# One accumulator instead of two for the routed experts: two scatter-adds in a row per expert tile

## The chip, the core and the metric

The kernel runs on one core of one Trainium2 chip. The core has a matmul engine (TensorE, PE in the rows, with its weight loads as PEld), a vector engine (VectorE, DVE), an activation engine (ScalarE, ACT), GpSimd (POOL) and SyncE (SP), which here only issues transfers. Sixteen DMA engines move data between the chip's memory (DRAM) and the on-chip memory (SBUF). Each engine runs its own instructions in order, and waits for others by semaphores. The metric is the device time of one execution in microseconds (us); less is better.

## The reference, cut to what matters

A backbone of two layers over 256 context and 256 latent tokens, D = 1024. Each layer has a token mixer and then a channel mixer: a shared expert for every token and 64 routed experts, of which each token goes to 8. Layer 0 routes all 512 tokens, layer 1 only the 256 latent ones, so 4096 and 2048 pairs of a token and an expert.

```python
TOP_K = 8; N_EXPERTS = 64; EXPERT_HIDDEN = 256

def swiglu(x, wg, wu, wd):
    return (jax.nn.silu(x @ wg) * (x @ wu)) @ wd
...
    # for every block of up to MOE_BLOCK rows of one expert e
    def block_ffn(args):
        tok, wt, e = args
        return swiglu(h_pad[tok], w_gate[e], w_up[e], w_down[e]) * wt[:, None]
    yb = lax.map(block_ffn, (...))
    return jax.ops.segment_sum(yb.reshape(n_rows, d), row_tok, num_segments=t + 1)[:t]
...
    routed = routed_experts(h, eidx, wts.astype(h.dtype), w_exp_gate, w_exp_up, w_exp_down)
    return routed + swiglu(h, w_sh_gate, w_sh_up, w_sh_down)
...
    h_lat = layer_norm(DN_ALPHA * h_lat + g2 * y_lat, ln2_g[l], ln2_b[l])
```

## The kernel before

Everything is float32. Outside of the routed experts a scheduler places the instructions of each engine; `experts` is written under a manual schedule, so its order is the order of the code.

**Routing** (`route`, L1240 on). The rows of an expert are cut into units of 64 rows, and two units make a tile of 128 rows. The first unit lies in partitions 0 to 63 (lane 0), the second in 64 to 127 (lane 1). A unit has as many rows with a token as its expert has left, up to 64; the others are empty. Tables give for each row of each tile the token to gather (`t_gather`) and the row of the accumulator to add to (`t_scatter`). The two units of a tile can hold the same token, for two experts. So the accumulator `acc` in DRAM has two halves of n + 64 rows, one for each lane. Row 0 to n - 1 of the first half are written by the shared expert (L980); the rest is filled with zeros from `zt` by transfers on ACT's queue (L1262). Empty rows add to spare rows, so that all 128 indices of a scatter are different and all are moved.

**The expert loop** (`experts`). For tile t, `body(t)` emits: transposes of the hidden values of tile t - 1 (`h_t`, L1586), gate and up products of tile t (L1577), the copies of the next weights out of a ring of four slots (`copies_gu` L1546, `copies_dn` L1552, on VectorE), the activation (L1581), transposes of the next tile's rows (`x_t`, L1568), the gather of tile t + 3 on GpSimd (L1526), and `down(t - 1)`: the down products (L1594), two ScalarE copies into `y` scaled by the routing weight (L1596), and a scatter-add of `y` into `acc` on GpSimd (L1597). There are two `y` buffers, used in turn, so `y` of tile t can be written once the scatter of tile t - 2 has landed. SyncE loads the next expert (three loads of 1 MB, L1227) when a slot is free, and signals landed loads (L1239).

All indirect transfers are GpSimd's, on queue q0; expert weights are on q1. A scatter-add reads its destination, so each waits until the scatter ahead of it has landed.

**The combine** (`combine`, L1643 on). For each 128 tokens SyncE loads both halves of `acc` (L1673), GpSimd adds them (L1675), VectorE multiplies and adds the residual (L1676, L1678), and a layer norm follows. In layer 0 the next mixer waits for it; in layer 1 it is the end of the program.

Of the kernel before, what the change touches and what calls it, by code (L numbers as in the profile page):

```python
# [60 lines left out]
def shape_consts():  # L61
# [6 lines left out]
    cols = [p]  # L68
    for n in (T, NLAT):
        pm, ln = p % UNIT, p // UNIT  # L70
        cols += [1 + n + pm, ln * (n + UNIT) + n + pm]
# [29 lines left out]
class Build:  # L101
# [37 lines left out]
    def rstd(self, pool, var, n, scale=1.0):  # L139
        """(scale * var + eps) ** -0.5 for [P, n]"""  # L140
        nc = self.nc
        ve = pool.tile([P, n], F32, name="rs_ve", bufs=4)
        nc.vector.tensor_scalar(ve, var, scale, LN_EPS, op0=ALU.mult, op1=ALU.add)  # L143
        r = pool.tile([P, n], F32, name="rs_r", bufs=6)
        nc.gpsimd.tensor_tensor(r, ve, self.eps[:, 1:2].to_broadcast([P, n]), op=ALU.pow)  # L145
        return r

    def ln_stats(self, pool, x, width):
        """rstd and -mean*rstd of x [P, width]"""
# [17 lines left out]
    def ln_sums(self, pool, x, sm, junk=None):  # L167
        """minus mean and rstd of x [P, D] from its sums"""
# [14 lines left out]
    def ln_two(self, pool, x, sm, g, b, out, total=None):  # L183
        """(x - mean) * rstd * g + b over [P, D], its sums to total"""
# [6 lines left out]
    def mod_prepare(self):  # L191
        """silu(c) of both streams, transposed: csT [P, KC, 32], column 0 context, 1 latent"""
# [20 lines left out]
    def mod_steps(self, l, i, rp, pool, bank):  # L213
        """columns 2048 i .. of silu(c) w_mod + b_mod; round 0 stays on chip transposed, the others go to DRAM"""
# [3 lines left out]
        for hf in range(2):  # L218
            # 256 columns to 32 rows of the product; a half of round 0 has half of the shifts and half of the scales
# [51 lines left out]
    def paced(self, steps):  # L271
        """steps of the background, behind the products so far"""
        with self.tc.issue_after(self.last):
            self.background(steps)

    def mod_bc(self, pool, l, which, s, name, bufs=None):
        """g1 / 2 0, sh2 1, 1 + sc2 2, g2 3 of stream s over all partitions"""
# [6 lines left out]
    def wload(self, w, n):  # L284
        """rows (k p) of a weight block [K, n] as [P, K / P, n]"""
# [6 lines left out]
    def fetch(self, dst, src):  # L292
        """a weight block, not ahead of the loads that the running phase waits for"""
# [4 lines left out]
    def order(self, i, after):  # L298
        """an instruction behind another one of its queue"""
# [3 lines left out]
    def wsplit(self, src):  # L303
        """float32 block [P, a, b] as two float32r parts"""
# [14 lines left out]
    def proj_T(self, pp, raw, j, xh, xl, t0, n):  # L319
        """transposed product of 128 columns j of a block: PSUM [P, n]"""  # L320
# [8 lines left out]
    def mixer_input(self, l, h_tiles, hs, pp, first=None, params=None):  # L329
        """uT hi / lo [P, KC, T]: modulated layer norm of both streams, transposed"""  # L330
# [45 lines left out]
    # per-row parameters (rows by partition), decay and angles of the S5 states: columns of one tile  # L376
# [7 lines left out]
    def params_load(self, sp, store):  # L384
        """the operands of mixer_params from DRAM"""
# [23 lines left out]
    def mixer_params(self, l, sp, pool, pp, store=None):  # L409
        """per-row parameters transposed, S5 discretisation and its block-diagonal operands; kept in sp, or sent to store"""  # L410
# [30 lines left out]
        # output rows by state, signs in them  # L441
# [32 lines left out]
        # powers 0 to 4 of the decay: re, im  # L474
# [14 lines left out]
        # by direction and pair of groups; backwards from 4 to 0  # L489
# [21 lines left out]
        # turns per chunk of 4 steps, and per 16 chunks  # L511
# [16 lines left out]
        # input rows by state  # L528
# [10 lines left out]
        # BP, input operands: blocks [4 steps of 32 channels, 128 states], the decay up to the end of the chunk in them  # L539
        # CK, output operands: the decay of 0 to 4 steps in them, backwards 4 to 0  # L540
        # W, products inside of a chunk: blocks [4 steps of 32 channels, 4 steps of 32 channels]
# [67 lines left out]
    def s5(self, l, pool, hp, pp, t0, n):  # L609
        """states; then ya^T / 2, hi and lo"""  # L610
# [5 lines left out]
        # in chunks of 4 steps; the states of the backward direction lie with the latents first  # L616
# [3 lines left out]
        hs = (c0 - 1, 1) if c0 else (0, 0)      # first state kept  # L620
        HH = []
        for k in range(2):
            H = []
            HH.append(H)
            for d in range(2):
# [36 lines left out]
                # states that are read: before each chunk in the order of the direction  # L662
# [12 lines left out]
        for k, H in enumerate(HH):  # L675
# [13 lines left out]
            # back to channels by token  # L689
# [16 lines left out]
    def attention(self, l, pool, pp, tiles, t0):  # L706
# [4 lines left out]
        # lambda  # L711
# [16 lines left out]
        for t in tiles:  # L728
# [4 lines left out]
            for h in range(NH):  # L733
# [13 lines left out]
                # the first map's sum divides the output  # L747
# [63 lines left out]
    def project(self, l, sp, pp, uh, ul, full):  # L811
        """a, k, q transposed; v and z by token"""
# [6 lines left out]
        for j in range(2):  # L819
            ps = self.proj_T(pp, raw, j, uh, ul, 0, T)  # L820
            nc.scalar.copy(self.aT[:, j, :], ps)
            # steps of a chunk next to each other on partitions
# [35 lines left out]
    def by_token(self, l, p, pp, uh, ul, base, tiles, name):  # L858
        """512 projected columns, tokens on partitions"""
# [16 lines left out]
    def behind(self, i, n):  # L876
        """products of step i of n spread over those of the attention"""
# [6 lines left out]
    def gates(self, l, pool, pp, uh, ul, t0, n, X, y, mT, steps, mh=None, ml=None):  # L884
        """adds a gated branch (0 S5, 1 gMLP, 2 attention) to mT, twice; the last one splits the sum, transposed [P, KC, n]"""
# [40 lines left out]
    def out_weights(self, l, hf, rp, wh, wl):  # L926
        """one half of the columns of w_out, split"""
# [23 lines left out]
    def shared_expert(self, pool, pp, fT, c0, w, dst):  # L951
        """in steps of a few products: gate, up, down"""
# [30 lines left out]
    def out_first(self, l, pool, tiles):  # L983
        """per-stream scale of the residual branch, sums and statistics of the tiles"""
# [8 lines left out]
    def residual(self, pool, half, t, hf, ps, h_tile):  # L993
        """half hf of the columns of ALPHA h + g1 mixer"""
# [8 lines left out]
    def out_proj(self, l, pool, pp, mh, ml, wh, wl, ps1, half, tiles, t0, h_tiles, h1_tiles, f_tiles, fT, rt):  # L1003
        """second half of the output projection, DeepNorm, modulated layer norm for the channel mixer"""
# [41 lines left out]
    def mixer(self, l, h_tiles, hs, keep, h1_tiles, f_tiles, outer, n, fD, acc):  # L1046
# [5 lines left out]
        with ExitStack() as ox:  # L1052
# [6 lines left out]
            with ExitStack() as cx:  # L1059
# [27 lines left out]
                with ExitStack() as lx:  # L1087
# [3 lines left out]
                    def mod_rounds():  # L1091
                        """the modulation vectors that are needed next, in the background"""
# [110 lines left out]
    def own(self, i, mine, other):  # L1203
        """accesses of the ring are ordered by two semaphores alone"""
# [7 lines left out]
    def load(self, l, raw, eid, cond, slot_off):  # L1212
        """expert weights into a slot of the ring"""
# [3 lines left out]
        for j, nm in enumerate(("w_exp_gate", "w_exp_up", "w_exp_down")):  # L1217
            w = self.A[nm][l][ds(e, 1)]
            src = w.rearrange("o (p k) n -> p (o k) n", p=P) if j < 2 else w.rearrange("o (k p) n -> p (o k) n", p=P)
# [23 lines left out]
    def route(self, l, n, rt, fD, acc, tab, raw, pool, pp):  # L1243
        """routing, the first weights, and the tables of the expert units"""
# [8 lines left out]
        # zero rows of the accumulator that the shared expert does not write  # L1253
# [3 lines left out]
        zt = pool.tile([P, D], F32, name="zt")  # L1257
        nc.gpsimd.memset(zt, 0.0)
        r0, r1 = n, LANES * (n + UNIT)
        while r0 < r1:  # L1260
            m = min(P, r1 - r0)
            nc.scalar.dma_start(acc[r0:r0 + m, :], zt[:m])  # L1262
            r0 += m
# [16 lines left out]
        for q in (slice(0, nt - 1), slice(nt - 1, nt)):  # L1280
# [7 lines left out]
            # rank of a group: groups above it, ties to the lower index  # L1288
# [19 lines left out]
        # counts: over the free axis (on every partition) and over partitions  # L1308
# [6 lines left out]
        # rows of an expert before a token  # L1315
# [14 lines left out]
        # columns: 0 units 1 active  # L1330
# [3 lines left out]
        # rank by count, then the order: largest, smallest, second largest, ...  # L1334
# [10 lines left out]
        tot = pool.tile([P, 4], F32, name="tot")       # units, active experts, half of them, 2 n - 1  # L1345
# [5 lines left out]
        for dst, src, q in ((ko[:, 0:NE], ps2[:, 0:NE], slice(0, P)), (c[:, 3:4], ps2[0:NE, NE:NE + 1], slice(0, NE))):  # L1351
            w = kt[q, 0:dst.shape[1]]
            # first half: 2 r, else 2 n - 1 - 2 r
# [19 lines left out]
        for k in range(SLOTS):  # L1373
            e, cnd = self.regs(tb["first"][0:1, 0:2, k], ET.SP)
            # few of them at a time: the gathers of the first tiles pass between them
# [6 lines left out]
        # tiles in use  # L1382
# [260 lines left out]
    def combine(self, l, stack, acc, h1_tiles, streams, out_tiles):  # L1643
# [6 lines left out]
        with tc.tile_pool(name="cbp", bufs=1, space=PSUM, reuse_waits="tile") as pp:  # L1650
# [13 lines left out]
            for t in range(2):  # L1664
                nc.sync.dma_start(tiles[t], h1_tiles[t])  # L1665
# [72 lines left out]
```

## Time and profile before

| | us |
|---|---|
| median of 3 runs (2009.78 to 2015.45) | 2012.02 |
| span of the profiled execution, first to last instruction (no other time is listed for it) | 2019.6 |
| first scatter of layer 0 to the landing of its last (43 tiles) | 524.2 |
| first scatter of layer 1 to the landing of its last (25 tiles) | 316.1 |

The profiled execution is 7.6 us (0.4%) longer than the median of the runs. PE is busy for 90% of the span, DVE for 58%, ACT for 30%, POOL for 26%. Such shares are means over stages with different limits; the two expert stages together are 840 us of the span, and each has to be read for itself.

### The profile page before, as it was taken

The numbers are of one execution on the slowest core, as the hardware profiler recorded it, in microseconds if no ns is written. First come the engines' busy times: TensorE is split into PE (matmuls) and PEld (weight loads), VectorE is DVE, ScalarE is ACT, GpSimd is POOL, SyncE is SP. The second block draws the span as 40 slices with busy tenths as digits, with TensorE's granted clock in tenths as the row PEclk, the third lists the DMA queues.
The fourth block names the chain that finished last, engine by engine and source line by source line (L and its number), as shares of the span: only waits on it lengthen the run. The fifth ranks groups of instructions, "written<-read, shape, count | busy, mean of one in ns | idle before, by whom it ended". The sixth has DMA issues, their size and how long they took to land. (4 is left out here: it accounts for less than half of the span.)

```text
span 2019.6 us, 31217 instructions
## 1 busy us (share of the span) xinstructions
PE 1815.0 (90%) x10521; PEld 1063.0 (53%) x10521; DVE 1178.6 (58%) x2346; ACT 595.8 (30%) x1139; POOL 527.3 (26%) x407
## 2 busy tenths in 40 slices
PE   4798999999999899999999973989989689998994
PEld 2686876677776333333333321777689543332331
DVE  7497544533475666666666547642564566665563
ACT  2343244432231222222222214423454212222211
POOL 4345400122210122222222214322042212222221
PEclk8899999999998999999999985988999799999986
DMA  8113333365677478778899957535553478999973
GB/s 273 48 43 91 134 111 120 128 211 177 231 266 273 126 222 275 226 211 282 260 338 314 373 157 271 201 128 189 192 175 123 189 285 276 332 327 386 378 265 110
DMA packets 168315, 440.18 MB, mean 218 GB/s; under 512 B 26262, under 2 KB 82996, under 8 KB 151227
## 3 DMA queue, kind: packets, MB, share of 16 engines
q1 hardware_dynamic: 132044, 340.89, 45.7%
q0 software_dynamic: 20448, 62.41, 13.5%
q10 hardware_dynamic: 15630, 34.56, 4.7%
q8 instruction: 90, 1.47, 0.3%
q14 instruction: 103, 0.84, 0.1%
HBM read 658.36 MB, written 58.17 MB: 355 GB/s over the span
## 5 line engine op out<-in xcount | busy, mean ns | idle before, releaser
L1577 PE MATMUL pg<-gu,xt 128*64 128x512 f32 x2176 | 498.2, 611 | 3.2 <-ACT xt L1569 2.7
L1546 DVE COPY gu<-raw 128x1024 f32 x560 | 364.4, 695 | 195.5 <-SPq L1239 87.2
L1577 PEld LDWEIGHTS pg<-gu,xt 128*64 128x64 f32 x2176 | 153.9, 140 | 299.9 <-issue 284.6
L1597 POOL DMA_INDIRECT acc<-y,t_scatter x68 | 125.0, 1838 | 607.8 <-ACT ht L1587 454.6
L1594 PE MATMUL py<-dn,ht 128*64 128x512 f32 x1088 | 250.2, 602 | 3.0 <-ACT ht L1587 3.0
L1552 DVE COPY dn<-raw 128x2048 f32 x140 | 172.2, 1230 | 123.9 <-PE py L1594 101.5
L135 PE MATMUL mm<-uh,whi 128*128 128x512 f32 (+1 forms) x544 | 198.5, 365 | 6.0 <-ACT rx L850 4.6
L137 PE MATMUL mm<-uh,wlo 128*128 128x512 f32 (+1 forms) x544 | 194.8, 358 | 1.7 <-POOL wlo L314 1.2
L136 PE MATMUL mm<-ul,whi 128*128 128x512 f32 (+1 forms) x544 | 194.8, 358 | 0.0
L314 DVE TENSOR_TENSOR wlo<-raw,whi 128x1024 fp32r<-128x1024 f32 x77 | 96.8, 1258 | 122.2 <-ACT whi L311 121.9
L1581 ACT ACTIVATE sg<-pg 128x256 f32<-128x256 f32 x68 | 26.3, 387 | 452.9 <-PE pg L1577 446.3
L1526 POOL DMA_INDIRECT xg<-f,t_gather x74 | 96.6, 1306 | 181.6 <-DVE lg L1489 62.9
L1596 ACT ACTIVATE y<-py,w 128x512 f32<-128x512 f32 x136 | 93.5, 688 | 159.9 <-PE py L1594 159.9
L1594 PEld LDWEIGHTS py<-dn,ht 128*64 128x64 f32 x1088 | 72.5, 137 | 129.2 <-issue 117.8
L311 ACT CAST whi<-raw 128x1024 fp32r<-128x1024 f32 x92 | 96.0, 1047 | 142.1 <-PE mm L136 113.3
L135 PEld LDWEIGHTS mm<-uh,whi 128*128 128x128 f32 x544 | 106.0, 195 | 32.5 <-issue 7.5
L137 PEld LDWEIGHTS mm<-uh,wlo 128*128 128x128 f32 x544 | 105.8, 195 | 20.6 <-issue 5.4
L136 PEld LDWEIGHTS mm<-ul,whi 128*128 128x128 f32 x544 | 106.1, 195 | 14.0 <-issue 1.8
L1568 PEld LDWEIGHTS px<-ct,xg 128*128 128x128 f32 x560 | 68.0, 194 | 56.1 <-issue 56.1
L1568 PE MATMUL px<-ct,xg 128*128 128x128 f32 x560 | 80.9, 287 | 0.0
L1569 ACT COPY xt<-px 128x512 f32<-128x512 f32 x140 | 75.3, 590 | 18.7 <-PE px L1568 16.8
L145 POOL TENSOR_TENSOR rs_r<-rs_ve,eps 128x1 f32<-128x1 f32 (+1 forms) x38 | 31.7, 837 | 166.1 <-DVE rs_ve L143 139.3
(473 smaller groups left out, 2795.4 us busy)
## 6 DMA issues: line engine op xcount, KB each, us to landing
raw<-in_w_exp_gate_dram SPq DMA_DIRECT2D x148, 1024.0 KB
raw<-in_w_exp_up_dram SPq DMA_DIRECT2D x148, 1024.0 KB
raw<-in_w_exp_down_dram SPq DMA_DIRECT2D x148, 1024.0 KB
raw<-in_w_in_dram SPq DMA_DIRECT2D x42, 1024.0 KB
mraw<-in_w_mod_dram SPq DMA_DIRECT2D x80, 512.0 KB
fraw<-in_w_mod_dram SPq DMA_DIRECT2D x16, 512.0 KB
cb_y<-acc SPq DMA_DIRECT2D x12, 512.0 KB
pj<-in_w_proj_da_dram SPq DMA_DIRECT2D x8, 512.0 KB
```

The source lines that it names most:

```text
L135: nc.tensor.matmul(out, lh, rh, start=start, stop=False)
L136: nc.tensor.matmul(out, lh, rl, start=False, stop=False)
L137: self.last = nc.tensor.matmul(out, ll, rh, start=False, stop=stop).ins
L311: self.nc.scalar.copy(hv, src)
L314: i = eng.tensor_tensor(lv, src, hv.bitcast(F32), op=ALU.subtract)
L1526: nc.gpsimd.indirect_dma_start(out=XG[t % AHEAD], out_offset=None, in_=fD, in_offset=bass.IndirectOffsetOnAxis(ap=tb["gather"][:, t:t + 1] ...
L1546: c = V.tensor_copy(GU[ln][b], gu[:, 2 * b:2 * b + 2])
L1552: c = V.tensor_copy(DN[ln][t % 2].rearrange("p a b -> p (a b)"), srcs[ln][:, 4096:6144])
L1568: nc.tensor.transpose(pX[hf][:, k * P:(k + 1) * P], XG[t % AHEAD][:, 4 * hf + k:D:8], ident)
L1577: nc.tensor.matmul(pG[t % 2][r, :], XT[t % 2][:, k, r], GU[ln][k // 2][:, k % 2].rearrange("p g n -> p (g n)"), start=(k == 0), stop=(k == ...
L1594: nc.tensor.matmul(pY[hf][r, :], HT[:, k, r], DN[ln][t % 2][:, k, 512 * hf:512 * hf + 512], start=(k == 0), stop=(k == 1), tile_position=( ...
L1597: nc.gpsimd.indirect_dma_start(out=acc, out_offset=bass.IndirectOffsetOnAxis(ap=tb["scatter"][:, t:t + 1], axis=0), in_=Y[t % 2], in_offse ...
```

## The change

Four things are done. The second half of the accumulator goes, with its zero fill and with the sum in the combine. Each tile is scattered twice, once with a table in which the rows of lane 1 are out of bounds, once with one in which those of lane 0 are; rows without a token are out of bounds in both. Out-of-bounds rows are skipped. The down weights are laid out so that each partition reads two neighbouring rows, 8 KB in one piece, and the transposes of the hidden values take every second column to match. Comments and docstrings are dropped too, so line numbers move (L1597 becomes L1586, L1673 becomes L1658).

```diff
@@ shape_consts
-    cols = [p]
-    for n in (T, NLAT):
-        pm, ln = p % UNIT, p // UNIT
-        cols += [1 + n + pm, ln * (n + UNIT) + n + pm]
+    cols = [p] + [4096 * (p // UNIT != ln) for ln in range(LANES)]
@@ load
-            src = w.rearrange("o (p k) n -> p (o k) n", p=P) if j < 2 else w.rearrange("o (k p) n -> p (o k) n", p=P)
+            src = w.rearrange("o (p k) n -> p (o k) n", p=P)
@@ route
-        zt = pool.tile([P, D], F32, name="zt")
-        nc.gpsimd.memset(zt, 0.0)
-        r0, r1 = n, LANES * (n + UNIT)
-        while r0 < r1:
-            m = min(P, r1 - r0)
-            nc.scalar.dma_start(acc[r0:r0 + m, :], zt[:m])
-            r0 += m
...
-        tb["gather"] = tab.tile([P, nx], I32, name="t_gather")
...
+        tb["tok"] = tab.tile([P, nx], I32, name="t_tok")
+        V.tensor_copy(tb["tok"], g)
+
+        tb["lane"] = [tab.tile([P, nx], I32, name="t_lane%d" % ln) for ln in range(LANES)]
+        for ln, x in enumerate(tb["lane"]):
+            V.tensor_scalar_add(v, g, self.C("pcol")[:, 1 + ln:2 + ln])
+            V.tensor_copy(x, v)
@@ experts
-                    nc.tensor.transpose(pH[:, k * P:(k + 1) * P], SG[t % 2][:, k * P:(k + 1) * P], ident)
+                    nc.tensor.transpose(pH[:, k * P:(k + 1) * P], SG[t % 2][:, k::2], ident)
...
-                nc.gpsimd.indirect_dma_start(out=acc, out_offset=bass.IndirectOffsetOnAxis(ap=tb["scatter"][:, t:t + 1], axis=0),
-                                             in_=Y[t % 2], in_offset=None, compute_op=ALU.add)
+                for ln in range(LANES):
+                    nc.gpsimd.indirect_dma_start(out=acc, out_offset=bass.IndirectOffsetOnAxis(ap=tb["lane"][ln][:, t:t + 1], axis=0),
+                                                 in_=Y[t % 2], in_offset=None, bounds_check=n - 1, oob_is_err=False, compute_op=ALU.add)
@@ combine
-            for t in range(2):
+            for t in range(len(streams)):
                 nc.sync.dma_start(tiles[t], h1_tiles[t])
...
-                y, y2 = (pool.tile([P, D], F32, name="cb_y%d" % i, bufs=4) for i in range(LANES))
-                if t >= 2:
-                    nc.sync.dma_start(tiles[t], h1_tiles[t])
-                for ln, a in enumerate((y, y2)):
-                    r = ln * (acc.shape[0] // LANES) + t * P
-                    self.urgent = nc.sync.dma_start(a, acc[r:r + P, :]).ins
+                y = pool.tile([P, D], F32, name="cb_y", bufs=4)
+                self.urgent = nc.sync.dma_start(y, acc[t * P:t * P + P, :]).ins
                 h = tiles[t]
-                G.tensor_tensor(y, y, y2, op=ALU.add)
@@ whole
-            acc = self.dram.tile([LANES * (n + UNIT), D], F32, name="acc%d" % l)
+            acc = self.dram.tile([n, D], F32, name="acc%d" % l)
```

GpSimd's order in the middle of layer 0's expert loop, before. A row names the line, the tile written and those read; DMASW0 to DMASW7 are the eight landing semaphores that GpSimd's transfers take in turn, and "Activation" is ScalarE's.

```order
L1526 DMA xg_5585<-f_94,t_gather 128x1088 [waits DMASW6_49,DVE_49,PE_49]
L1597 DMA acc_95<-y_6146,t_scatter 1152x1024 [waits DMASW3_49,Activation_49]
L1526 DMA xg_5586<-f_94,t_gather 128x1088 [waits DMASW0_49,DVE_49,PE_49]
L1597 DMA acc_95<-y_6147,t_scatter 1152x1024 [waits DMASW5_49,Activation_49]
L1526 DMA xg_5587<-f_94,t_gather 128x1088 [waits DMASW2_49,DVE_49,PE_49]
L1597 DMA acc_95<-y_6146,t_scatter 1152x1024 [waits DMASW7_49,Activation_49]
```

There a gather and a scatter alternate, and a scatter waits for ScalarE's `y` and for the scatter ahead of it, two rows up. The same place of the change:

```order
L1513 DMA xg_5586<-f_94,t_tok 128x1088 [waits DVE_49,PE_49]
L1586 DMA acc_95<-y_6139,t_lane_5950 512x1024 [waits DMASW7_49,Activation_49]
L1586 DMA acc_95<-y_6139,t_lane_5951 512x1024 [waits DMASW2_49,DMASW1_49]
L1513 DMA xg_5587<-f_94,t_tok 128x1088 [waits DVE_49,PE_49]
L1586 DMA acc_95<-y_6140,t_lane_5950 512x1024 [waits DMASW2_49,Activation_49]
L1586 DMA acc_95<-y_6140,t_lane_5951 512x1024 [waits DMASW5_49,DMASW4_49]
```

Now the second scatter of a tile (`t_lane_5951`, lane 1; the first such row here takes DMASW2) stands right behind the first (which takes DMASW1), and waits for DMASW1, that is, for the first to have landed. The first scatter of the next tile waits for DMASW2. The gather of a later tile stands behind both.

SyncE's order at the start of layer 0's combine, before (`cb_h` is the residual, `cb_y` a part of the accumulator):

```order
L1665 DMA cb_h_13468<-h_0_93 128x1024
L1673 DMA cb_y_13473<-acc_95 128x1024 [waits DMASW6_49,DMASW5_49,DMASW7_49,DMASW4_49,DMAHW6_49,DMASW2_49,DMASW0_49]
L1673 DMA cb_y_13474<-acc_95 128x1024 [waits DMAHW0_49]
L1673 DMA cb_y_13494<-acc_95 128x1024 [waits DMAHW2_49]
L1673 DMA cb_y_13495<-acc_95 128x1024 [waits DMAHW3_49]
L1670 DMA cb_h_13469<-h_0_93 128x1024 [waits DMAHW4_49]
```

And of the change:

```order
L1654 DMA cb_h_13941<-h_0_93 128x1024
L1654 DMA cb_h_13942<-h_0_93 128x1024 [waits DMAHW1_49]
L1654 DMA cb_h_13943<-h_0_93 128x1024 [waits DMAHW3_49]
L1658 DMA cb_y<-acc_95 128x1024 [waits DMASW5_49,DMASW4_49,DMASW6_49,DMASW3_49,DMASW7_49,DMASW2_49,DMAHW5_49,DMASW1_49,DMASW0_49]
L1658 DMA cb_y<-acc_95 128x1024 [waits DMAHW6_49]
```

All residual loads now stand ahead of the loads that wait for the scatters, and there is one load of the accumulator per 128 tokens where there were two.

## Rows read from the trace of the kernel before

**Rows 1.** The page's head: span, busy us and share by engine

```profile
span 2019.6 us, 31217 instructions
PE 1815.0 (90%) x10521; PEld 1063.0 (53%) x10521; DVE 1178.6 (58%) x2346; ACT 595.8 (30%) x1139; POOL 527.3 (26%) x407
```

**Rows 2.** Busy time by stretch: both scatter stages, and layer 0's thinnest 50 us

```profile
core 0: us, PE busy (x) PEld busy (x) DVE busy (x) ACT busy (x) POOL busy (x), PEclk, DMA share, GB/s
686.90:1211.10 524.20, 507.81 (x2397) 186.10 (x2394) 334.68 (x535) 129.05 (x249) 129.45 (x85) 0.98 0.80 260
1674.00:1990.10 316.10, 287.66 (x1348) 104.43 (x1344) 187.20 (x301) 73.61 (x140) 79.33 (x48) 0.96 0.91 314
...
1150.00:1200.00 50.00, 38.21 (x162) 13.53 (x160) 24.22 (x39) 9.62 (x18) 9.08 (x5) 0.89 0.65 214
```

**Rows 3.** The same two stages, of the scatter's line alone

```profile
686.90:1211.10 524.20, 76.32 (x43) 0.98 0.80 260
1674.00:1990.10 316.10, 48.64 (x25) 0.96 0.91 314
```

**Rows 4.** Timeline of one tile in layer 0: start, us, engine, line, names

```profile
801.87 0.39 ACT L1581 ACTIVATE sg<-pg 128x256 f32<-128x256 f32 x1 [6.41 <-PE pg L1577]
...
806.57 0.69 ACT L1596 ACTIVATE y<-py,w 128x512 f32<-128x512 f32 x1 [1.05 <-PE py L1594]
...
807.54 1.80 POOL L1597 DMA_INDIRECT acc<-y,t_scatter  x1 [8.65 <-ACT ht L1587]
...
809.64 1.31 POOL L1526 DMA_INDIRECT xg<-f,t_gather  x1 [0.30 <-issue]
...
813.93 0.39 ACT L1581 ACTIVATE sg<-pg 128x256 f32<-128x256 f32 x1 [6.41 <-PE pg L1577]
```

**Rows 5.** Who waited for whom: VectorE's copies for loads of weights

```profile
DVE gu L1546 <- SPq L1239: 87.2, 26, 9.3
```

**Rows 6.** Timeline, layer 0's last scatter, and the load that waits for it

```profile
1204.78 1.57 POOL L1597 DMA_INDIRECT acc<-y,t_scatter  x1 [7.52 <-ACT y L1596]
...
1211.10 2.75 SPq L1673 DMA_DIRECT2D cb_y<-acc  x4
```

**Rows 7.** DMA queues, 1206.8 to 1210.8 us: packets, MB, share of 16 engines

```profile
q0 software_dynamic: 144, 0.52, 82.2%
```

**Rows 8.** Timeline of POOL: a scatter of layer 0 among weight loads

```profile
1036.68 1.80 POOL L1597 DMA_INDIRECT acc<-y,t_scatter  x1 [8.65 <-ACT ht L1587]
```

**Rows 9.** DMA queues behind it: 1036.7 to 1041.9, then 1041.9 to 1047.6 us

```profile
q1 hardware_dynamic: 402, 1.98, 99.5%
...
q1 hardware_dynamic: 171, 1.26, 55.6%
q0 software_dynamic: 156, 0.56, 48.1%
```

**Rows 10.** Queue q0 in 668.9:670.6, 740.5:742.7, 840.0:843.9 and 853.1:857.0: gathers

```profile
q0 software_dynamic: 107, 0.20, 35.0%
...
q0 software_dynamic: 169, 0.59, 75.7%
...
q0 software_dynamic: 149, 0.27, 17.7%
...
q0 software_dynamic: 160, 0.57, 35.9%
```

**Rows 11.** Timeline of layer 1's combine: VectorE's residual step, beside GpSimd's sum and alone

```profile
2004.04 2.39 DVE L1678 SCALAR_TENSOR_TENSOR cb_h<-cb_h,cb_y 128x1024 f32<-128x1024 f32 x1
...
2009.21 1.22 DVE L1678 SCALAR_TENSOR_TENSOR cb_h<-cb_h,cb_y 128x1024 f32<-128x1024 f32 x1
```

**Rows 12.** All combine tiles by line: GpSimd's sum, VectorE's residual step

```profile
L1675 POOL TENSOR_TENSOR cb_y<-cb_y,cb_y 128x1024 f32<-128x1024 f32 x6 | 14.0, 2341 | 21.7 <-DMA cb_y<-acc 21.7
L1678 DVE SCALAR_TENSOR_TENSOR cb_h<-cb_h,cb_y 128x1024 f32<-128x1024 f32 x6 | 13.1, 2181 | 0.1
```

**Rows 13.** Timeline of ACT while layer 0's accumulator is filled with zeros

```profile
594.35 0.59 ACT L979 COPY sh_y<-sh_ps 128x512 f32<-128x512 f32 x1 [3.30 <-DMA acc<-zt]
```

More of the change, by code (lines that the diff above doesn't have):

```diff
@@ L1477, in route @@
                 nc.tensor.matmul(pl[:, 0:nx], oa[:, j, :], ob[:, j, :], start=(t == 0 and j == 0), stop=(t == nt - 1 and j == 7))
-        pcc = self.C("pcol")
-        k1 = 1 if n == T else 3
         v = pool.tile([P, nx], F32, name="lv")
@@ L1484, in route @@
         V.scalar_tensor_tensor(g, v, -1.0, g, op0=ALU.add, op1=ALU.add)
-        tb["gather"] = tab.tile([P, nx], I32, name="t_gather")
-        V.tensor_copy(tb["gather"], g)
-        V.tensor_scalar(g, v, 0.5, None, op0=ALU.is_gt)
-        V.tensor_scalar(g, g, pcc[:, k1:k1 + 1], -1.0, op0=ALU.mult, op1=ALU.mult)
-        V.tensor_scalar(g, g, pcc[:, k1 + 1:k1 + 2], None, op0=ALU.add)
-        V.tensor_add(g, g, v)
-        tb["scatter"] = tab.tile([P, nx], I32, name="t_scatter")
-        V.tensor_copy(tb["scatter"], g)
+        tb["tok"] = tab.tile([P, nx], I32, name="t_tok")
[4 more added lines that the diff above has]
+            V.tensor_copy(x, v)
         return tb
@@ L1526, in gather @@
                 nc.gpsimd.indirect_dma_start(out=XG[t % AHEAD], out_offset=None, in_=fD,
-                                             in_offset=bass.IndirectOffsetOnAxis(ap=tb["gather"][:, t:t + 1], axis=0),
+                                             in_offset=bass.IndirectOffsetOnAxis(ap=tb["tok"][:, t:t + 1], axis=0),
                                              bounds_check=n - 1, oob_is_err=False)
```

## The prediction

> **What bounds the kernel now.** I read the page's head first, then the busy time by stretch, the timelines of one tile and of GpSimd, the list of who waits for whom, and the DMA queues in short windows around single scatters. The reader should see in the head that PE is busy for 90% of the span [rows 1]. The change, though, sits in two stages and in the work right before and behind them, so these are read apart. From the first scatter's issue to the last one's landing layer 0 takes 524.2 us and layer 1 316.1 us [rows 2]. They have 43 and 25 scatters [rows 3], so a tile takes 524.2/43 = 12.19 us and 316.1/25 = 12.64 us. Where nothing disturbs, ScalarE's activation comes every 813.93 − 801.87 = 12.06 us, each time after a wait for PE [rows 4]: PE sets the pace. 43 × 12.06 = 518.6 and 25 × 12.06 = 301.5, so other waits cost 5.6 us in layer 0 and 14.6 us in layer 1. What they are stands in the list of waits: VectorE's copies of the next weights wait 87.2 us for loads [rows 5], of which about 20 us reach PE. The DMA engines are busy for 80% of layer 0's stage and 91% of layer 1's [rows 2].
>
> So PE is the bound, and the scatter is hidden. It has room: `y` lies in two buffers, so a scatter may take until ScalarE writes that buffer again, nearly two tiles later; but as each scatter waits for the one ahead of it, all scatters together may take no more than 12.06 us per tile on average. One scatter, from issue to landing, takes 1211.10 − 1204.78 = 6.3 us where the queues are otherwise empty [rows 6]; its packets pass in the last 4.0 us of that [rows 7], 2.0 us go by before the first. Among loads of weights it takes 11.2 us: issue at 1036.68 [rows 8], then no packet of its queue until 1041.9, while the loads hold 99.5% of the engines, and packets until 1047.6, that is for 5.7 us [rows 9]; 0.3 us I count for the landing signal. It held 48.1% of 16 engines for 5.7 us, or 2.7 us of all of them. The weights go on moving meanwhile.
>
> **The change part by part.** *Two scatters in a row.* The second waits for the first to land, and the next tile's first waits for the second. A tile's chain of scatters is therefore two landings long, and what counts is whether a scatter of half the rows lands in half the time. No half scatter stands in this trace. From both sides: its transfer takes as long as a whole one's (1.0), or half as long (0.5); the time before the first packet stays in both. The nearest rows are gathers of few and of many rows in the same stretch of the program. On empty queues a gather of 0.20 MB (some 47 rows with a token, of 4.35 KB each) moves for 1.7 us and one of all 128 for 2.2 us, a ratio of 0.77; among loads one of 0.27 MB (some 62 rows) takes 3.9 us, as one of all 128 does, a ratio of 1.0 [rows 10]. They are nearer to 1.0 than to 0.5. I take 0.8, since of 64 rows in a lane some are empty too and are now skipped: 6144 pairs on 2 × 68 lanes are 45 rows in each.
>
> That gives a landing of 6.3 − 0.2 × 4.0 = 5.5 us on empty queues and 11.2 − 0.2 × 5.7 = 10.1 us among loads, for two 11.0 and 20.2. How often it meets loads follows from the other DMA work of a tile, W: the busy share of a tile less the scatter, 0.80 × 12.19 − 2.7 = 7.05 us in layer 0, 0.91 × 12.64 − 2.7 = 8.8 us in layer 1. If the chain sets the tile time T, the loads hold W/T of it, and T = 11.0 + 9.2 × W/T, an estimate from these rows. Solved, T = 15.2 us in layer 0 and 16.0 us in layer 1. (The same for one whole scatter gives 6.3 + 4.9 × 7.05/12.19 = 9.1 us: hidden, as now.) Both are above 12.06, so the chain becomes the bound: 43 × (15.2 − 12.19) = +130 us and 25 × (16.0 − 12.64) = +84 us, together **+214 us**. The load waits of 20 us go in that, since loads have more time.
>
> What is queued behind the waiting scatters on GpSimd is the gather of a tile three ahead (1.31 us of POOL time, [rows 4]). It is late by no more than the chain, and has three tiles of slack. ScalarE's write of `y` is late next: it waits in front of the transposes' copy and of the next activation on the same engine, and so stops PE through its full PSUM buffers.
>
> *Second accumulator.* GpSimd's sum takes 2341 ns each [rows 12] and stands once per layer between the last load and VectorE: −4.7 us. The second load per 128 tokens is 0.52 MB; at layer 1's 314 GB/s for a share of 0.91 [rows 2] that is 0.52/345, about 1.5 us, once per layer: −3.0. VectorE's residual step takes 2.39 us while GpSimd adds beside it and 1.22 us alone [rows 11]; six take 2181 ns on average [rows 12], so 6 × (2.18 − 1.22) = −5.8 us. ScalarE's copy of the shared expert waits 3.3 us behind the issue of the zero fill [rows 13]; others beside it have cover by PE, so I take −2. Sum: about **−15 us**. With these hidden it would be 0, and the range holds that.
>
> *Transposes and down weights.* Transposes that read every second column are as many as before; those of `xg` take eight-column strides already at PE's pace. The down weights arrive in pieces of 8 KB where they came in 4 KB: the loads' share can fall a little, behind the chain. Both at nothing. Were the cover gone, a twentieth of W (0.4 us per tile) would move T by 0.2 us, 15 us in all.
>
> Sum: 214 − 15 = +199 us on the profiled 2019.6. That execution is 7.6 us over the median, which I take off: **2211 us**.
>
> **Rivals.** *A half scatter transfers as long as a whole one.* The gathers among loads speak for it (3.9 and 3.9 us), the ones on empty queues against it. With 12.6 + 9.8 × W/T: T = 16.7 and 17.5 us, 43 × 4.5 + 25 × 4.9 = +316, less 15: **2313 us**. Chance 0.22. [...]
>
> *Half the rows, half the transfer.* 4.3 and 8.35 us; 8.6 + 8.1 × W/T gives 13.0 and 13.8 us: 43 × 0.8 + 25 × 1.2 = +64, less 15: **2061 us**. For it: a scatter is one packet stream whose bytes halve. Against it: the gather rows. Chance 0.15.
>
> *The other side: the landing falls with the rows that are moved.* Then 45 rows cost 45/128 of the transfer, 2.3 + 0.35 × 4.0 = 3.7 us on empty queues and 5.5 + 0.35 × 5.7 = 7.5 us among loads; 7.4 + 7.6 × W/T is 11.9 us in layer 0, below PE's 12.06, and 12.7 us in layer 1. The chain stays hidden, the combine's 15 us are won, and skipped rows ease the loads: 8704 − 6144 = 2560 rows × 2.7/128 = 54 us of 16 engines, against 20 us of waits. **1977 to 1997 us.** It decides where a landing is at most 12.06/2 = 6.03 us on average. A whole one on empty queues takes 6.3 us, and the queues are not empty, so the chance is 0.12.
>
> *PE's clock as the bound.* It could fall where PE waits more: in layer 0's thinnest 50 us PE was granted 0.89 of full speed with 38.2 of 50 us busy [rows 2]. A tile at 12.06/0.89 = 13.5 us is still under 15.2, so the clock changes nothing in the likeliest case.
>
> **How the numbers follow.** Likeliest, between the first two bounds: 0.45, at 2150 to 2270 by itself (a ratio of 0.65 to 0.9, the combine's gain kept or not). Whole 0.22 at 2313, half 0.15 at 2061, other side 0.12 at 1977 to 1997, and 0.06 in between, where the chain just touches PE's pace (2005 to 2045). Reaching from just under the half case to just over the whole one, 2040 to 2330 leaves out the other side and part of the last, under 2 in 10. No change is within 0.3%, about what this kernel's measurement tells apart: 6 us. Faster has 0.12, same 0.05 (part of the in-between), slower 0.83.
>
> **What would show it.** Stages of about 650 and 400 us; an activation every 15 to 16 us; GpSimd waiting for the first scatter's landing ahead of each second one and ScalarE's `y` waiting for a landing; PE's share in the stages near 0.75 to 0.8; few VectorE waits for weights. In the combine no sum, residual steps of 1.2 us. If instead the activation still comes every 12.06 us and ScalarE's `y` waits for PE, the landing was mis-sized and the other side holds. A landing that stays at 6.3 us or more on empty queues shows the whole case, one near 4.3 the half case.

## The result, and the profile after

The changed kernel takes 2254.1 us (median of 4 runs, 2251.3 to 2262.6) where before takes 2013.7 us: a ratio of 1.119, with a 95% interval of 1.115 to 1.124. It is slower, as forecast, and inside of the range; 2211 us was 43 us too low. The page's head of its profiled execution stands against [rows 1]:

```profile
span 2249.4 us, 31515 instructions
PE 1857.6 (83%) x10521; PEld 1088.5 (48%) x10521; DVE 1181.8 (53%) x2344; ACT 586.2 (26%) x1139; POOL 636.9 (28%) x467
```

PE has 43 us more of busy time and POOL 110, but the span is 230 us longer: no engine works that much more, they wait. The busy time by stretch shows where (columns as in [rows 2]; each stretch from the first scatter's issue to the landing of the last, read off the combine's load that waits for it; in layer 1 of before that load comes 3.2 us behind the landing, which ends the stretch there):

```profile
683.08:1366.11 683.03, 539.16 (x2397) 202.38 (x2394) 339.61 (x535) 122.85 (x248) 215.89 (x128) 0.89 0.60 194
1816.08:2227.40 411.32, 305.06 (x1349) 114.54 (x1346) 191.35 (x301) 70.19 (x140) 119.86 (x74) 0.86 0.68 232
```

| stretch | before, us | after, us | difference |
|---|---|---|---|
| up to the first scatter | 686.9 | 683.1 | −3.8 |
| scatters of layer 0 | 524.2 | 683.0 | +158.8 |
| between the stages | 462.9 | 450.0 | −12.9 |
| scatters of layer 1 | 316.1 | 411.3 | +95.2 |
| behind the last landing | 29.5 | 22.0 | −7.5 |
| span | 2019.6 | 2249.4 | +229.8 |

The loss, 254 us, lies in the two stages: 683.0/43 = 15.9 us and 411.3/25 = 16.5 us per tile where 15.2 and 16.0 were forecast. Everything outside of them got 24 us shorter. (The medians differ by 240 us, 10 more than these two executions, whose spans lie 6 us above the median before and 5 us below it after.) The DMA engines, busy for 0.80 and 0.91 of the stages before, are now so for 0.60 and 0.68, and PE for 0.79 and 0.74: none of these is busy all the time in the stages. The timeline of GpSimd says what they wait for (start, us, engine, line, names, idle time before and what ended it):

```profile
764.39 1.58 POOL L1586 DMA_INDIRECT acc<-y,t_lane  x1 [8.19 <-DMA acc<-y,t_lane]
770.83 1.55 POOL L1586 DMA_INDIRECT acc<-y,t_lane  x1 [4.86 <-DMA acc<-y,t_lane]
772.69 1.06 POOL L1513 DMA_INDIRECT xg<-f,t_tok  x1 [0.30 <-issue]
777.87 2.13 POOL L1586 DMA_INDIRECT acc<-y,t_lane  x1 [4.12 <-DMA acc<-y,t_lane]
785.45 1.56 POOL L1586 DMA_INDIRECT acc<-y,t_lane  x1 [5.46 <-DMA acc<-y,t_lane]
```

Scatter, landing, scatter, landing: 6.4, 7.0 and 7.6 us apart here, each issue 0.6 to 1.3 us behind the last packet of the scatter ahead of it. In the list of who waited for whom, the scatters' landings now lead:

```profile
POOL acc L1586 <- DMA acc<-y,t_lane: 653.3, 121, 10.1
ACT y L1583 <- DMA acc<-y,t_lane: 553.3, 51, 19.7
...
PE px L1555 <- DMA xg<-f,t_tok: 176.9, 33, 10.9
...
DVE gu L1533 <- SPq L1236: 12.0, 10, 4.2
```

None of the first three was in that list before. The reader should see both ways in which the chain reaches PE: ScalarE can't write `y`, and the gather that stands behind two waiting scatters on GpSimd comes late. VectorE's waits for weights fell from 87.2 us [rows 5] to 12.0, since the loads have time now. The timeline of ScalarE shows one tile:

```profile
811.15 1.26 ACT L1583 ACTIVATE y<-py,w 128x512 f32<-128x512 f32 x2 [16.07 <-DMA acc<-y,t_lane]
812.31 0.37 ACT L1574 COPY ht<-ph 128x256 f32<-128x256 f32 x1
812.56 0.40 ACT L1568 ACTIVATE sg<-pg 128x256 f32<-128x256 f32 x1
...
828.22 0.38 ACT L1568 ACTIVATE sg<-pg 128x256 f32<-128x256 f32 x1 [2.41 <-PE pg L1564]
```

Two activations are 15.66 us apart, 12.06 before [rows 4], and ahead of `y` ScalarE waited 16.07 us for a landing.

I split the chain by the packets of queue q0 in the trace (means, us; a skipped row appears there as a packet of 8 bytes and 8 ns):

| scatters | number | issue to first packet | first to last packet | last packet to next scatter's issue |
|---|---|---|---|---|
| before, layer 0 (128 rows moved) | 43 | 3.45 | 4.73 | 4.10 (waits for `y`) |
| before, layer 1 | 25 | 4.16 | 4.90 | 3.72 (waits for `y`) |
| after, layer 0 | 86 | 3.24 | 3.71 | 1.00 |
| of these, 64 rows moved | 51 | 3.24 | 4.20 | 0.99 |
| of these, up to 16 rows moved | 14 | 3.24 | 2.16 | 1.09 |
| after, layer 1 | 50 | 3.52 | 3.72 | 1.00 |

The three parts of a scatter add up to the stage in any kernel with one scatter behind the other (here 86 × (3.24 + 3.71 + 1.00) = 684 us and 50 × 8.24 = 412 us), so it is the last column that tells: about 1.0 us in both layers and for thick and thin scatters, and never over 2.4, where before it is 4 us of waiting for `y`. So GpSimd hardly ever waited for `y` instead of a landing: the chain of landings sets the length of both stages, and PE doesn't.

A full lane's transfer on empty queues is as long as that of a whole tile. DMA queue q0 behind the scatter issued at 764.39, from 766.5 to 770.3 us (packets, MB, share of 16 engines):

```profile
q0 software_dynamic: 144, 0.26, 49.5%
```

Half the bytes of [rows 7] in 3.8 us in place of 4.0, at 49.5% of the engines in place of 82.2%. It is no single case: where other packets held under 2% of the engines meanwhile, all 38 scatters of 64 rows took 3.4 to 4.0 us, and the 13 whole tiles of before 3.4 to 3.9.

The combine's rows against [rows 11, 12]: no sum on GpSimd, and VectorE's residual step never slowed.

```profile
L1662 DVE SCALAR_TENSOR_TENSOR cb_h<-cb_h,cb_y 128x1024 f32<-128x1024 f32 x6 | 7.3, 1220 | 0.1
```

### The profile page after: what moved, and what is told of

It reads as the page before. It is cut to its first block, busy times and chain, and to the rows that moved or that the text cites. A ratio compares the mean times of both kernels' runs of the same rounds, so it can differ in the third digit from the quotient of the medians.

```text
span 2249.4 us, 31515 instructions
## 1 busy us (share of the span) xinstructions
PE 1857.6 (83%) x10521; PEld 1088.5 (48%) x10521; DVE 1181.8 (53%) x2344; ACT 586.2 (26%) x1139; POOL 636.9 (28%) x467
## 5 line engine op out<-in xcount | busy, mean ns | idle before, releaser
L1564 PE MATMUL pg<-gu,xt 128*64 128x512 f32 x2176 | 484.0, 597 | 3.1 <-ACT xt L1556 3.1
L1586 POOL DMA_INDIRECT acc<-y,t_lane x136 | 245.2, 1803 | 754.5 <-DMA acc<-y,t_lane 653.3
L1581 PE MATMUL py<-dn,ht 128*64 128x512 f32 x1088 | 285.4, 672 | 13.8 <-ACT ht L1574 13.7
L1583 ACT ACTIVATE y<-py,w 128x512 f32<-128x512 f32 x136 | 86.8, 684 | 652.9 <-DMA acc<-y,t_lane 553.3
L1555 PE MATMUL px<-ct,xg 128*128 128x128 f32 x560 | 99.0, 331 | 176.9 <-DMA xg<-f,t_tok 176.9
L1555 PEld LDWEIGHTS px<-ct,xg 128*128 128x128 f32 x560 | 81.3, 202 | 235.3 <-DMA xg<-f,t_tok 208.0
L1581 PEld LDWEIGHTS py<-dn,ht 128*64 128x64 f32 x1088 | 80.7, 155 | 176.2 <-issue 144.8
L1513 POOL DMA_INDIRECT xg<-f,t_tok x74 | 103.2, 1395 | 162.9 <-DVE lv L1478 96.4
L1569 DVE TENSOR_TENSOR sg<-sg,pg 128x256 f32<-128x256 f32 x68 | 28.1, 413 | 107.6 <-ACT sg L1568 107.6
```

The source lines that it names most:

```text
L1513: nc.gpsimd.indirect_dma_start(out=XG[t % AHEAD], out_offset=None, in_=fD, in_offset=bass.IndirectOffsetOnAxis(ap=tb["tok"][:, t:t + 1], a ...
L1555: nc.tensor.transpose(pX[hf][:, k * P:(k + 1) * P], XG[t % AHEAD][:, 4 * hf + k:D:8], ident)
L1564: nc.tensor.matmul(pG[t % 2][r, :], XT[t % 2][:, k, r], GU[ln][k // 2][:, k % 2].rearrange("p g n -> p (g n)"), start=(k == 0), stop=(k == ...
L1581: nc.tensor.matmul(pY[hf][r, :], HT[:, k, r], DN[ln][t % 2][:, k, 512 * hf:512 * hf + 512], start=(k == 0), stop=(k == 1), tile_position=( ...
L1586: nc.gpsimd.indirect_dma_start(out=acc, out_offset=bass.IndirectOffsetOnAxis(ap=tb["lane"][ln][:, t:t + 1], axis=0), in_=Y[t % 2], in_offs ...
```

## The experiments

The theory: the time is that of a chain of landings, two per tile, since each scatter into one accumulator waits for the one ahead. Rivals: the second scatter costs by its work (issue on GpSimd, packets), the two `y` buffers couple PE and scatters too tightly, or another part of the change made the stages long. Two accumulators, one scatter, four `y` buffers and skipping alone ran on one chip, the other four on a second one, each beside runs of before (2022 and 2023 us there), so ratios are to be compared.

**Two accumulators.** The two scatters stay and stop waiting for each other. (Not shown: the second accumulator's place in DRAM and its filling with zeros.)

```diff
-                    nc.gpsimd.indirect_dma_start(out=acc, ...
+                    nc.gpsimd.indirect_dma_start(out=acc[ln], ...
...
-                y = pool.tile([P, D], F32, name="cb_y", bufs=4)
-                self.urgent = nc.sync.dma_start(y, acc[t * P:t * P + P, :]).ins
+                y, y2 = (pool.tile([P, D], F32, name="cb_y%d" % i, bufs=4) for i in range(LANES))
+                for a, b in zip((y, y2), acc):
+                    self.urgent = nc.sync.dma_start(a, b[t * P:t * P + P, :]).ins
...
+                G.tensor_tensor(y, y, y2, op=ALU.add)
```

> The change with one edit: each lane's scatter adds into an accumulator of its own, the second one filled with zeros and summed up in the combine as before. Still two scatters of 128 indices per tile with skipped rows, but the two of a tile no longer wait for each other. Chain theory (the time is two landings in a row per tile): a lane's chain is one landing of about 7 us and 1 us to the next issue, under PE's 12.06 us, so the stages fall back to about 525 and 316 us and the time to 2000 to 2020 us. Work theory (a second issue of 1.8 us and 128 more packets per tile are what costs): the stages stay at 650 us or more and 400 us, the time above 2200 us.

Measured: 2012.0 us, a ratio to before of 0.995 (0.992 to 0.998). The stages by stretch, and the timeline of GpSimd in layer 1:

```profile
681.98:1212.60 530.62, 515.87 (x2403) 192.44 (x2400) 335.44 (x535) 128.65 (x248) 207.60 (x128) 0.98 0.75 250
1670.13:1984.00 313.87, 287.47 (x1350) 107.12 (x1347) 189.33 (x301) 73.13 (x140) 120.32 (x74) 0.97 0.85 301
```

```profile
1670.13 1.62 POOL L1590 DMA_INDIRECT acc<-y,t_lane  x1 [10.80 <-ACT ht L1578]
1672.05 1.88 POOL L1590 DMA_INDIRECT acc<-y,t_lane  x1 [0.30 <-issue]
1674.23 1.26 POOL L1517 DMA_INDIRECT xg<-f,t_tok  x1 [0.30 <-issue]
1682.07 1.81 POOL L1590 DMA_INDIRECT acc<-y,t_lane  x1 [6.58 <-ACT ht L1578]
```

GpSimd has 208 and 120 us of work where the change has 216 and 120, the second scatter is issued 0.3 us behind the end of the first one's issue, and 250 of the 254 us are gone. The work theory falls; the wait between the scatters is the cause.

**One scatter.** The rest of the change, without the second scatter. (Not shown: the tables' code and the size of the accumulator.)

```diff
-    cols = [p] + [4096 * (p // UNIT != ln) for ln in range(LANES)]
+    cols = [p] + [n * (p // UNIT) for n in (T, NLAT)]
...
-                for ln in range(LANES):
-                    nc.gpsimd.indirect_dma_start(out=acc, out_offset=bass.IndirectOffsetOnAxis(ap=tb["lane"][ln][:, t:t + 1], axis=0),
-                                                 in_=Y[t % 2], in_offset=None, bounds_check=n - 1, oob_is_err=False, compute_op=ALU.add)
+                nc.gpsimd.indirect_dma_start(out=acc, out_offset=bass.IndirectOffsetOnAxis(ap=tb["lane"][0][:, t:t + 1], axis=0),
+                                             in_=Y[t % 2], in_offset=None, bounds_check=LANES * n - 1, oob_is_err=False, compute_op=ALU.add)
```

> The change with one scatter of 128 rows per tile in place of two, empty rows skipped, lane 1 adding to rows behind the first n that the combine never reads: the sums of lane 1 are left out of the result. The combine, the routing and the down weights are those of the change. Chain theory: one landing of 8 to 9 us is hidden behind PE's 12.06 us; the stages are at or a little below those of before (505 to 524 and 302 to 316 us), and outside of them the 24 us stay won, so 1970 to 1992 us. If something else in the change (the strided transposes, the 8 KB pieces, the new order) makes the stages long, they stay above 540 and 330 us.

Measured: 1996.4 us, 0.987 (0.983 to 0.991). By stretch:

```profile
689.56:1211.10 521.54, 508.49 (x2399) 190.72 (x2396) 334.30 (x535) 128.72 (x248) 130.48 (x85) 0.99 0.75 251
1665.80:1975.30 309.50, 290.42 (x1355) 107.80 (x1352) 187.64 (x301) 73.15 (x140) 76.54 (x49) 0.98 0.89 317
```

The stages are as expected; nothing else in the change lengthens them. The whole is 4 us above what I expected; in its profiled execution the first scatter starts 6.5 us later than the change's, and why stays open. All that the change does beside the second scatter is worth 1.3%, in a kernel that leaves the sums of lane 1 out of the result; the second scatter turns it into a loss of 11.9%.

**Four `y` buffers.**

```diff
-            Y = [pool.tile([P, D], F32, name="y%d" % i) for i in range(2)]
+            Y = [pool.tile([P, D], F32, name="y%d" % i) for i in range(4)]
...
-                                                 in_=Y[t % 2], in_offset=None, bounds_check=n - 1, oob_is_err=False, compute_op=ALU.add)
+                                                 in_=Y[t % 4], in_offset=None, bounds_check=n - 1, oob_is_err=False, compute_op=ALU.add)
```

> The change with four buffers for y in place of two, so that ScalarE may write y of a tile before the scatters two tiles back have landed. Chain theory: the scatters follow each other without a gap already, so a deeper queue in front of them changes nothing: 2245 to 2265 us, with GpSimd's waits for landings as long and ScalarE's waits for them gone or moved to PE's wait for gathered rows, which are queued on GpSimd behind the scatters. Buffer theory (the two y buffers couple PE and scatters and lose time at each tile): the stages shorten by a tenth or more, below 2170 us.

Measured: 2254.4 us, 1.114 (1.110 to 1.119), the change's time within the intervals. The stages are 685.9 and 414.5 us long (683.0 and 411.3 in the change). Who waited for whom:

```profile
POOL acc L1586 <- DMA acc<-y,t_lane: 621.8, 112, 11.5
...
ACT y L1583 <- PE py L1581: 198.3, 134, 3.8
PE px L1555 <- DMA xg<-f,t_tok: 178.0, 35, 11.0
```

ScalarE's 553 us of waits for landings are gone from the list and the stages are no shorter: those waits were a symptom. PE still waits for gathered rows, which the same chain holds back. The buffer theory falls.

**Other halves.** Why does half a scatter take so long? The same two scatters in a row, cut by 32 partitions. (Not shown: the choice of the table's column by layer.)

```diff
-    cols = [p] + [4096 * (p // UNIT != ln) for ln in range(LANES)]
+    cols = [p] + [4096 * (p // 32 % 2 != ln) + n * (p // UNIT) for n in (T, NLAT) for ln in range(LANES)]
...
-                                                 in_=Y[t % 2], in_offset=None, bounds_check=n - 1, oob_is_err=False, compute_op=ALU.add)
+                                                 in_=Y[t % 2], in_offset=None, bounds_check=LANES * n - 1, oob_is_err=False, compute_op=ALU.add)
...
-            acc = self.dram.tile([n, D], F32, name="acc%d" % l)
+            acc = self.dram.tile([LANES * n, D], F32, name="acc%d" % l)
```

> The change with the two scatters of a tile cut another way: the first takes the rows of partitions 0 to 31 and 64 to 95, the second those of 32 to 63 and 96 to 127. So that no two rows of a scatter hit the same row, those of lane 1 go to rows behind the first n that the combine never reads: the sums of lane 1 are left out of the result. As many issues, rows and waits as in the change. Half-of-the-engines theory (a lane's 64 partitions are served by 8 of 16 DMA engines, so its transfer takes as long as one of 128): here each scatter has rows on all 16, its transfer of full tiles falls from 3.6 us towards 1.8 us on empty queues, a landing from 7.0 to about 5.2 us, a tile to 12.4 to 13.2 us, and the time to 2015 to 2060 us. Rival (the transfer follows the rows or bytes of a scatter, however they lie): 2240 to 2265 us as in the change.

Measured: 2182.8 us, 1.079 (1.074 to 1.084) against the change's 1.119: faster than the change, and over 120 us slower than I expected. The stages, and queue q0 from 753.3 to 755.6 us behind a scatter of 64 rows on an otherwise nearly empty queue:

```profile
691.74:1309.80 618.06, 524.11 (x2395) 197.06 (x2392) 336.68 (x535) 124.80 (x248) 217.42 (x128) 0.93 0.67 215
1763.12:2166.20 403.08, 307.03 (x1351) 115.75 (x1348) 189.38 (x301) 70.43 (x140) 124.95 (x74) 0.88 0.71 245
```

```profile
q0 software_dynamic: 144, 0.26, 81.8%
```

The theory of half of the engines fits: the same 0.26 MB pass in 2.3 us at 81.8% of the engines, where the change took 3.8 us at 49.5%. In the change's trace a scatter of 36 to 64 rows has most often 8 packets of 4 KB in flight at a time, in the trace of before a whole tile has 16 (all 48 and 12 of 13 where other packets held under 2% of the engines). The trace doesn't name a packet's engine, so which partitions an engine serves is not shown; the rows of each scatter show what the time depends on. Where other packets held under 2% of the engines, the change's scatters of 11 to 32 rows took 2.1 to 2.3 us and those of 36 to 64 rows 3.1 to 4.0, while with the other halves those of 11 to 64 rows all took 2.0 to 2.5. A unit's rows fill its lane from the first partition on, so the step comes where rows lie in the second 32 partitions of a lane as well as in the first; the cut by 32 never has both in one scatter. How the rows lie sets the transfer, not only how many they are.

The size that I forecast for the other cut was wrong, for I let every transfer shrink: by the packets the mean falls from 3.71 to 2.87 us in layer 0 and from 3.72 only to 3.34 in layer 1, and the time to the first packet stays (3.29 and 3.72). Where other packets held half of the engines or more, full scatters of layer 0 took 3.8 to 5.3 us, and the change's 4.8 to 5.9. In layer 1 the two means are also of other scatters: 9 of 64 rows and 3 of up to 16, where the change has 20 and 10.

**Skipping empty rows alone**, in the kernel before.

```diff
-        cols += [1 + n + pm, ln * (n + UNIT) + n + pm]
+        cols += [4097 - ln * (n + UNIT), np.full(P, 4096)]
...
-                                             in_=Y[t % 2], in_offset=None, compute_op=ALU.add)
+                                             in_=Y[t % 2], in_offset=None, bounds_check=LANES * (n + UNIT) - 1, oob_is_err=False, compute_op=ALU.add)
```

> The kernel before with one edit: rows without a token have an index out of bounds and are skipped, 2560 of 8704. Still one scatter per tile and two halves of the accumulator. If skipping frees the DMA engines (54 us of all 16 over the two stages), the waits of VectorE for weights get shorter and the time falls by up to 20 us, to 1994 to 2010 us. If landings are hidden and the loads wait for slots rather than for the engines, nothing: 2008 to 2018 us. If the 8-byte packets of skipped rows cost more than the rows, it is slower than 2020 us.

Measured: 2004.3 us, 0.991 (0.988 to 0.994): faster by 0.9%, in the range of the first of the three. The wait of [rows 5]:

```profile
DVE gu L1546 <- SPq L1239: 56.7, 19, 8.1
```

30 us less of waits for weights. In the profiled executions the stages are 4.2 and 7.8 us shorter (520.0 and 308.3 us); another 10 us of their difference lie outside of the stages, and I can't tell them from the spread of single executions.

**Down weights in 8 KB pieces alone**, with the transposes.

```diff
-            src = w.rearrange("o (p k) n -> p (o k) n", p=P) if j < 2 else w.rearrange("o (k p) n -> p (o k) n", p=P)
+            src = w.rearrange("o (p k) n -> p (o k) n", p=P)
...
-                    nc.tensor.transpose(pH[:, k * P:(k + 1) * P], SG[t % 2][:, k * P:(k + 1) * P], ident)
+                    nc.tensor.transpose(pH[:, k * P:(k + 1) * P], SG[t % 2][:, k::2], ident)
```

> The kernel before with the down weights in 8 KB pieces and the transposes of every second column alone. My prediction put both at nothing: 2005 to 2028 us beside a before of 2013 to 2022. Rival: fewer, larger pieces free the DMA engines and shorten VectorE's waits for weights of 87 us, 10 us or more faster.

Measured: 2011.3 us, 0.996 (0.994 to 0.999). A gain of some 0.4% (0.1 to 0.6%), where I had nothing; the rival's 10 us lie inside of the interval too. VectorE's wait for weights is 75.5 us.

**Both side edits together** (the two diffs above in the kernel before).

> The kernel before with both side edits of the change and without the rest: rows without a token skipped, down weights in 8 KB pieces. If they ease the same waits for weights, no more than skipping alone (0.9% faster); if they add up, 1.2% or more.

Measured: 2008.3 us, 0.993 (0.990 to 0.996). They don't add up by these runs, though VectorE's wait for weights is the shortest of all with 46.5 us. The intervals of skipping alone and of both overlap; which is better stays open.

**The sum on VectorE**, with empty rows skipped.

```diff
-                G.tensor_tensor(y, y, y2, op=ALU.add)
+                V.tensor_add(y, y, y2)
```

> The kernel before with rows without a token skipped, and the sum of the two halves in the combine on VectorE (a VectorE pass of this size takes 1.22 us) in place of GpSimd (2.34 us, and VectorE's residual step beside it 2.2 to 2.4 us in place of 1.22). If the combine's gain in the change was GpSimd's sum and its slowing of VectorE, this gives 3 to 8 us beyond skipping alone, at 1.1 to 1.3% below before; if it was the second load, nothing beyond 0.9%.

Measured: 1998.5 us, 0.988 (0.984 to 0.992), the lowest ratio of those that compute all of the reference. The combine's rows by line:

```profile
L1675 DVE TENSOR_TENSOR cb_y<-cb_y,cb_y 128x1024 f32<-128x1024 f32 x6 | 7.3, 1221 | 42.0 <-DMA cb_y<-acc 42.0
L1678 DVE SCALAR_TENSOR_TENSOR cb_h<-cb_h,cb_y 128x1024 f32<-128x1024 f32 x6 | 7.3, 1220 | 0.1
```

The sum costs 1.22 us in place of 2.34, and the residual step is back at 1.22. In ratio that is 0.3 points beyond skipping alone, on another chip and inside of both intervals: the rows are shown, the gain in time isn't.

## Why the prediction held, and where it was off

**The bound.** Right. PE set the pace and hid one landing; two in a row became the bound in both layers, and the time lies in the range of that branch (2150 to 2270). Two accumulators gave back 250 of 254 us.

**The landing of half a scatter.** The value taken, 0.8 of a whole transfer, was about right as a mean over the stages: 3.71/4.73 = 0.78 and 3.72/4.90 = 0.76. That mean has emptier queues than before in it; at like load the ratio is 3.21/3.64 = 0.88 (others under 2% of the engines) and 4.52/5.49 = 0.82 (others half of them or more). And it is not one kind of scatter: on empty queues a full lane took as long as a whole tile, and a lane of 11 to 32 rows 2.1 to 2.3 us, somewhat over half of that. So the rival of the whole transfer was right for full lanes, and the rival of the half transfer nearly so for lanes up to 32 rows. The rival of the moved rows was right for neither: it gives 32 rows 1.0 us. That the mix came to 0.8 was in part luck: the gathers that the value was taken from don't show what sets it.

**What was mis-sized.** Two terms of the sum. First, "0.3 us I count for the landing signal": that is SyncE's release. GpSimd takes 1.00 us on average from the last packet to its next issue; in layer 0 it is 0.78 us on average ahead of a tile's second scatter and 1.23 us ahead of the next tile's first. That is 0.7 us more per scatter, or 1.4 us per tile. Second, issue to last packet was 7.0 and 7.2 us where the estimate gave 7.3 and 7.7 (half of 15.2 and 16.0, less 0.3), which gives back 0.7 and 0.9 us per tile. Together 15.9 and 16.5 us for 15.2 and 16.0, some 40 us in all.

**What is late next.** ScalarE's `y` was late as I said (553.3 us of waits for landings). That the gather "has three tiles of slack" was wrong: PE waited 176.9 us for gathered rows. It cost nothing, for with or without ScalarE's waits the chain was full, as four buffers showed.

**The combine.** −15 us forecast, −24 measured between the profiled executions outside of the stages (−3.8, −12.9, −7.5). The rows for the sum and the residual step came as forecast (2181 to 1220 ns). Some 3 of the remaining 9 us stand in the traces of layer 1: before, SyncE issues the load of the accumulator 3.9 us behind the last scatter's last packet (at 1993.35, behind residual loads at 1992.28), in the change 0.4 us behind it. Where the rest comes from stays open; one scatter is 15 us shorter than before outside of the stages, so it may be how the scheduler placed other work.

**Side edits at nothing.** Not quite: the down weights in 8 KB pieces, put at nothing, gain 0.4% alone in the kernel before, and skipping rows gains 0.9%; in both VectorE waits less for weights (75.5 and 56.7 us for 87.2). That the chain hides both in the change, as the sum had it, is argued and was not run: there VectorE waits 12.0 us for weights in all.

**PE's clock.** With PE waiting, the granted clock fell from 0.98 and 0.96 to 0.89 and 0.86 in the stages (means over stretches granted 1.0 and others granted 0.5, which are 3.4 to 28.5 us long in the change), and PE's busy time rose by 31 and 17 us in them. As the last column of the chain's table shows no wait for `y`, it set nothing.

## What to carry to other kernels

Before cutting a transfer in two that must follow each other, add up what doesn't shrink with it: here 3.2 to 3.5 us to the first packet and 1.0 us from the last packet to the next issue, of 8 us from one issue to the next. The rest need not shrink with the rows either: here 64 rows took 3.7 us on empty queues where they filled a lane, as a whole tile does, and 2.3 where the cut took them from both lanes. A hidden chain stays free only up to the pace of what hides it, so compare the sum of its landings with that pace (here 16 with 12.06 us). And when several engines show long waits on one thing, remove one of the waits: if the time stands, it was a symptom of the chain.

## What was not expected of the hardware

Skipped rows are not absent: 11264 of 17408 rows of the change's scatters appear as packets of 8 bytes, but at 8 ns each against 328 ns for one of 4 KB (medians) they cost next to nothing. A scatter cut by partitions 0 to 63 and 64 to 127 keeps the 16 engines busy for 49.5%, as half of them would be, one cut by 32 partitions for 81.8%, and a whole tile's for 82.2%. On empty queues that takes the transfer of 64 rows from 3.7 to 2.3 us on average, and a lane's first 32 rows alone take 2.3 us as well. In layer 1, where the DMA engines are busy for 0.68 to 0.71 of the stage, the mean falls only from 3.72 to 3.34.
